# Feed-forward blocks by seven block products instead of eight, with the weight sums shared between VectorE and the DMA engines

## The chip, the cores and the metric

The kernel runs on one core of a Trainium2 chip. The metric is the device time of one execution in microseconds, the median of several. Matmuls run on TensorE (PE, with PEld for its weight loads); VectorE (DVE), ScalarE (ACT) and GpSimd (POOL) work on tiles of up to 128 partitions; SyncE (SP) issues most DMA transfers. Each engine takes its instructions in the order of the program and waits on semaphores for the others.

## The reference

One layer with 512 tokens, a width of 1024 and a feed-forward width of 2816, all in float32:

```python
def swiglu(x, w_gate, w_up, w_down):
    return (jax.nn.silu(x @ w_gate) * (x @ w_up)) @ w_down
...
    for l in range(DEPTH):
        h = rms_norm(x, norm_ffn1[l])
        x = x + 0.5 * swiglu(h, ffn1_gate[l], ffn1_up[l], ffn1_down[l])
        h = rms_norm(x, norm_mix[l])
        p = h @ w_in[l]
        ...                       # o_rwkv: a linear recurrence; o_attn: attention in a window of 128
        mixed = jnp.concatenate([o_rwkv.astype(x.dtype), o_attn.astype(x.dtype)], axis=-1)
        x = x + mixed @ w_out[l]
        h = rms_norm(x, norm_ffn2[l])
        x = x + 0.5 * swiglu(h, ffn2_gate[l], ffn2_up[l], ffn2_down[l])
    return rms_norm(x, norm_final)
```

The two feed-forward blocks, a before the mixer and b behind it, hold most of the arithmetic.

## The kernel before

A float32 product is made of three matmuls in a faster format (float32r): both factors are split into a high and a low part, and hi·hi, hi·lo and lo·hi are added up in PSUM (`mm3`, lines 455 to 457). x lies transposed, with channels on the partitions, so that eight tiles of 128x512 hold it and its split (`split_act`, 320 and 321).

A block runs over 22 columns f of 128 hidden channels. For each, gate and up take 24 matmuls apiece: the weights (128x128) are stationary and all 512 tokens move (`ffn`, 462 to 510). `gated` (516 to 520) makes silu(gate) times up, which is split again (317, 318). The down projection comes in three parts of 8, 8 and 6 hidden tiles, and adds into x from PSUM (508). The last part of block b runs in the layout of the output, with the hidden tiles stationary and the weights moving (`finish`, 548 to 550), and the last norm follows there piece by piece (553 to 569).

Weights come by SP into three raw tiles of 512 KB (`weights_load`, 402); ACT makes the high part (409) and DVE the low part (410), one or two tiles ahead of their use, driven by a list (`make_plan`, `want`, `take`). At the start, x's tiles are transposed by PE as they land (233) and products of the first column stand between the transposes (252). Statistics of the norms are matmuls of one column (341), a power by GpSimd (344) and a spread over the partitions by PE (350, 352). In the mixer, x is put away to DRAM and fetched again by GpSimd's queue (595, 601).

Of the kernel before, what the change touches and what calls it, by code (L numbers as in the profile page):

```python
# [5 lines left out]
F32 = mybir.dt.float32  # L6
# [4 lines left out]
P = 128  # L11
# [14 lines left out]
MAN = {PE, ACT, DVE}  # L26
AHEAD = 2
SPREAD = 13
MS = 8
# [7 lines left out]
MPOOL = False  # L37
MAN1 = {PE}
# [12 lines left out]
w.5.1 wd.6.1 a.4 m.7.1 zd.4 t.6 oe.3 we.5 ah.4 wd.5.1 w.7.0 u.4 ux al.4 bp.1 uv.4 te.6 g.1 wd.5.0 w.7.1 bo.1 t.5 ud.4  # L51
we.7 s.4 wd.7.0 te.5 o.4 wd.7.1 a.6 oe.4 n.4.0 ge.1 a.5 n.4.1 ah.6 q.1 t.7 al.6 ah.5 b.6 wh.0 gb.1 z.5 al.5 te.7 var.1
# [3 lines left out]
wo.5.1 wl.3 wo.4.0 xa.5 ns.3 wo.7.0 ht.3 wo.4.1 mg.3 wo.7.1 wh.4 xa.4 mh.3 wl.4 wo.6.0 ml.3 wo.6.1 xa.7 xa.6  # L56
"""
PARTS = [(0, 8), (8, 16), (16, 22)]
# [3 lines left out]
KEEP = "rg"  # L62
PACK = 1792 + 768 + 512 * sum({"r": 4, "v": 4, "g": 1, "e": 1, "O": 4, "V": 1, "w": 8}[x] for x in KEEP)
DECAY = math.exp(-0.5)

class Net:
    def __init__(self, ctx, tc, I, out):
# [10 lines left out]
        self.m2 = pool(name="m2", bufs=2)  # L78
        self.dram = pool(name="dram", bufs=1, space=bass.MemoryType.DRAM)
# [22 lines left out]

    def keep(self, x, name):
        return self.const(S) if x in KEEP else self.tile2(name)

    def consts(self):
        nc, I = self.nc, self.I
        cp = self.cp
        self.pack = cp.tile([P, PACK], F32, name="pack")
# [13 lines left out]
    def first_gain(self):  # L123
        nc = self.nc
        pt = self.psum("gain1_ps")
# [4 lines left out]
    def vectors(self):  # L130
        """The vectors over channels, one column per 128 of them."""
# [24 lines left out]
        pt = self.psum("vec_ps")  # L156
# [4 lines left out]
    def consts_mix(self):  # L161
        nc, I, cp = self.nc, self.I, self.cp
        c = self.col["mix"]
# [5 lines left out]
        # per-head one-hot columns and the block of ones per head  # L169
# [8 lines left out]
        # takes the mean of each head's channels off  # L178
        self.cent = self.const(P)
        nc.vector.scalar_tensor_tensor(self.cent, self.blk, -1.0 / 64, self.ident, ALU.mult, ALU.add)  # L180
        # [s, 0, t] = t > s; [s, 1, t] = t >= s, s = partition mod 64
# [7 lines left out]
        # 0 at the first step of each chunk  # L189
# [3 lines left out]
        # window mask  # L193
# [13 lines left out]
    def start(self, x):  # L207
        """Loads x, transposes it and makes the first operands, and the products of the first tile of the first ffn."""
        nc = self.nc
        with self.tc.manual_schedule(engines={PE, ACT, DVE, mybir.EngineType.SP}):  # L210
            self.warm()
            raws, ws = [], []
            for j in range(ND):
                if j % 2 == 0:
                    xin = self.tile4(f"xin{j}", (P, 2, 4, P))
                raws.append(xin[:, j % 2])
                nc.sync.dma_start(raws[j], x[0, :, j * P:(j + 1) * P].rearrange("(t p) c -> p t c", p=P))
                if j < 4:
                    self.first_load(ws)
# [1104 lines left out]
```

## Time and profile before

| | us |
|---|---|
| median of three runs | 1022.75 |
| lowest and highest run | 1021.14, 1022.91 |
| span of the profiled execution, first to last instruction | 1023.7 |
| PE busy in it | 1008.6 |
| DVE busy | 557.8 |
| ACT busy | 397.5 |
| POOL busy | 52.2 |

The profile is of one execution; its span is 0.95 us over the median of the runs. Shares of the page's 40 slices and its table of engines are averages over stages with different limits: block a lies from 0 to about 384 us, the mixer to about 665, block b to the end.

### The profile page before, as it was taken

The numbers are of one execution on the slowest core, as the hardware profiler recorded it, in microseconds if no ns is written. First come the engines' busy times: TensorE is split into PE (matmuls) and PEld (weight loads), VectorE is DVE, ScalarE is ACT, GpSimd is POOL, SyncE is SP. The second block draws the span as 40 slices with busy tenths as digits, with TensorE's granted clock in tenths as the row PEclk, the third lists the DMA queues.
The fourth block names the chain that finished last, engine by engine and source line by source line (L and its number), as shares of the span: only waits on it lengthen the run. The fifth ranks groups of instructions, "written<-read, shape, count | busy, mean of one in ns | idle before, by whom it ended". The sixth has DMA issues, their size and how long they took to land. (4 is left out here: it accounts for less than half of the span.)

```text
span 1023.7 us, 12876 instructions
## 1 busy us (share of the span) xinstructions
PE 1008.6 (99%) x5123; PEld 824.8 (81%) x5123; DVE 557.8 (54%) x886; ACT 397.5 (39%) x631; POOL 52.2 (5%) x84
## 2 busy tenths in 40 slices
PE   8999999999999999999999999999999999999997
PEld 6888888888888887888867788788888888888886
DVE  5644424444344568799976686644443444424445
ACT  5422212332222447864376754432222322212343
POOL 6000000000000010120010120000000000000001
PEclk8999999999999999999989899999999999999999
DMA  8333333333233352313230323223333333333322
GB/s 207 103 101 87 100 103 92 94 103 101 85 102 93 103 176 62 94 51 78 77 84 22 93 63 103 81 87 101 102 97 88 103 101 88 101 103 90 96 83 83
DMA packets 174444, 96.82 MB, mean 95 GB/s; under 512 B 12334, under 2 KB 170096, under 8 KB 174384
## 3 DMA queue, kind: packets, MB, share of 16 engines
q1 hardware_dynamic: 172032, 90.19, 30.9%
q0 software_dynamic: 2336, 5.81, 2.0%
q8 instruction: 40, 0.66, 0.3%
q14 instruction: 20, 0.16, 0.1%
q10 hardware_dynamic: 16, 0.00, 0.0%
HBM read 89.43 MB, written 4.19 MB: 91 GB/s over the span
## 5 line engine op out<-in xcount | busy, mean ns | idle before, releaser
L457 PE MATMUL bpgu<-h_o,lo_bg 128*128 128x512 f32 x176 | 69.3, 394 | 0.0
L455 PE MATMUL bpgu<-h_o,hi_bg 128*128 128x512 f32 x176 | 69.2, 393 | 0.0
L456 PE MATMUL bpgu<-h_o,hi_bg 128*128 128x512 f32 x176 | 69.0, 392 | 0.0
L455 PE MATMUL apd<-h_a,hi_ad 128*128 128x512 f32 x176 | 68.6, 390 | 0.0
L456 PE MATMUL apd<-h_a,hi_ad 128*128 128x512 f32 x176 | 68.5, 389 | 0.0
L457 PE MATMUL apd<-h_a,lo_ad 128*128 128x512 f32 x176 | 68.5, 389 | 0.0
L457 PE MATMUL bpgu<-h_o,lo_bu 128*128 128x512 f32 x176 | 68.5, 389 | 0.0
L455 PE MATMUL bpgu<-h_o,hi_bu 128*128 128x512 f32 x176 | 68.5, 389 | 0.0
L456 PE MATMUL bpgu<-h_o,hi_bu 128*128 128x512 f32 x176 | 68.5, 389 | 0.0
L457 PE MATMUL apgu<-h_x,lo_au 128*128 128x512 f32 x168 | 65.5, 390 | 0.0
L455 PE MATMUL apgu<-h_x,hi_ag 128*128 128x512 f32 x168 | 65.5, 390 | 0.0
L455 PE MATMUL apgu<-h_x,hi_au 128*128 128x512 f32 x168 | 65.4, 390 | 0.0
L456 PE MATMUL apgu<-h_x,hi_au 128*128 128x512 f32 x168 | 65.4, 389 | 0.0
L457 PE MATMUL apgu<-h_x,lo_ag 128*128 128x512 f32 x168 | 65.4, 389 | 0.0
L456 PE MATMUL apgu<-h_x,hi_ag 128*128 128x512 f32 x168 | 65.4, 389 | 0.0
L409 ACT ACTIVATE hi_bu<-raw_bu 128x1024 fp32r<-128x1024 f32 x22 | 23.4, 1061 | 87.0 <-PE bpgu L456 78.3
L409 ACT ACTIVATE hi_au<-raw_au 128x1024 fp32r<-128x1024 f32 x21 | 22.3, 1062 | 83.0 <-PE apgu L456 70.1
L516 DVE TENSOR_TENSOR sgb<-bpgu,rstd 128x512 f32<-128x512 f32 x22 | 15.2, 692 | 70.6 <-PE bpgu L457 69.4
L516 DVE TENSOR_TENSOR sga<-apgu,rstd 128x512 f32<-128x512 f32 x22 | 15.2, 691 | 69.2 <-PE apgu L457 66.4
L409 ACT ACTIVATE hi_ad<-raw_ad 128x1024 fp32r<-128x1024 f32 (+1 forms) x24 | 23.8, 991 | 74.9 <-PE apd L456 51.9
L455 PE MATMUL bpd<-h_b,hi_bd 128*128 128x512 f32 x128 | 49.8, 389 | 0.0
L456 PE MATMUL bpd<-h_b,hi_bd 128*128 128x512 f32 x128 | 49.8, 389 | 0.0
(427 smaller groups left out, 2348.3 us busy)
## 6 DMA issues: line engine op xcount, KB each, us to landing
raw_bg<-in_ffn_gate_dram SPq DMA_DIRECT2D x22, 512.0 KB, 3.8
raw_bu<-in_ffn_up_dram SPq DMA_DIRECT2D x22, 512.0 KB, 3.8
raw_ag<-in_ffn_gate_dram SPq DMA_DIRECT2D x21, 512.0 KB, 3.9
raw_au<-in_ffn_up_dram SPq DMA_DIRECT2D x21, 512.0 KB, 3.8
raw_ad<-in_ffn_down_dram SPq DMA_DIRECT2D x16, 512.0 KB, 4.0
raw_bd<-in_ffn_down_dram SPq DMA_DIRECT2D x16, 512.0 KB, 4.0
raw_o<-in_w_out_dram SPq DMA_DIRECT2D x16, 256.0 KB, 3.3
raw_ad<-in_ffn_down_dram SPq DMA_DIRECT2D x8, 384.0 KB, 3.6
```

Of the source, the lines that this page charges most:

```text
L409: nc.scalar.activation(hi[:, :n], raw[:, :n], AF.Copy)
L455: nc.tensor.matmul(ps, hi[:, k], ah, start=first, stop=False)
L456: nc.tensor.matmul(ps, hi[:, k], al, start=False, stop=False)
L457: nc.tensor.matmul(ps, lo[:, k], ah, start=False, stop=last)
L516: nc.vector.tensor_tensor(sg, pg, self.rstd, ALU.mult)
```

## The change

Both blocks are rewritten. Tokens and both other dimensions are halved, and each product of 2x2 blocks is made by seven block products (M1, M7, M2, M6, M5, M3, M4 in this order) of sums of blocks, in the form that accumulates in PSUM. Activations are stationary (128x128) and weights move, 512 columns at a time (256 in the last of six column blocks). For gate and up, the two block columns are up and gate, and the two block rows are the halves of the 1024 channels; a product has two pieces of 128x1024 weights, and each takes 12 matmuls. The hidden rows come out with tokens on the partitions; PE turns them (`hidden_turn`). The down part runs each product over six pieces.

`Stream` replaces the list of weights. `loads` issues the plain loads, by SP, and for three of four weight blocks of down by GpSimd's queue. A weight sum is made in place in a raw tile: `add` is a transfer from DRAM that accumulates, `add_here` an addition by DVE. Activation sums are additions by GpSimd. x now lies in rows (`xN`); for the mixer it is transposed by `turn_rows` in `tail_a` and `between`, at the start by `operand_turn`, and the output projection of the mixer has the activations stationary too.

```diff
+PRODUCTS = ("M1", "M7", "M2", "M6", "M5", "M3", "M4")
+LOADS, LOADS_D, HIGH, LOW, HI, LO = 9, 5, 3, 2, 5, 4
...
+    def add(self, pc, b, i, j):
+        self.nc.gpsimd.dma_start(self.raw[pc.kind, pc.c, pc.idx, b], pc.block(i, j), accum_op=ALU.add)
+
+    def add_here(self, pc, b, other):
+        a, o = (self.raw[pc.kind, pc.c, pc.idx, x] for x in (b, other))
+        self.nc.vector.tensor_tensor(a, a, o, ALU.add)
...
+            b = {"M1": "11", "M7": "12", "M2": "21", "M3": "22"}.get(pc.m)
+            if b:
+                eng = self.nc.gpsimd if pc.kind == "d" and pc.m != "M3" else by or self.nc.sync
+                eng.dma_start(self.tile(pc, b), pc.block(int(b[0]) - 1, int(b[1]) - 1))
+            if pc.m == "M7":
+                self.add(pc, "12", 1, 1)
...
+            self.nc.scalar.activation(hi, raw, AF.Copy)
...
+            self.nc.vector.tensor_tensor(lo, raw, hi.bitcast(F32), ALU.subtract)
+            self.parts[pc.q] = hi, lo
+            if pc.m == "M7":
+                self.add_here(pc, "12", "11")
+                self.add(pc, "11", 0, 1)
+            elif pc.m == "M6" and pc.kind == "gu":
+                self.add_here(pc, "12", "21")
+            elif pc.m == "M6":
+                self.add(pc, "12", 1, 0)
...
+    def mm3w(self, ps, ah, al, bh, bl, first, last):
+        mm = self.nc.tensor.matmul
+        mm(ps, ah, bh, start=first, stop=False, skip_group_check=True)
+        mm(ps, al, bh, start=False, stop=False, skip_group_check=True)
+        mm(ps, ah, bl, start=False, stop=last, skip_group_check=True)
...
+        for f in range(nf):
+            nc.tensor.transpose(pt[:, f], h[:, f * P:(f + 1) * P], self.ident)
+        nc.scalar.activation(self.hT[c][:, :, t * P:(t + 1) * P], pt, AF.Copy)
...
+        if pc.m == "M7":
+            self.ds[pc.c] = self.f.tile([P, 2, 256], F32, tag="ds", name=f"ds{pc.q}", bufs=5)[:, :pc.nk]
+            eng.tensor_tensor(self.ds[pc.c], a11, a21, ALU.subtract)
+        elif pc.m == "M6":
+            eng.tensor_tensor(a21, a22, a21, ALU.subtract)
+            eng.tensor_tensor(a11, a11, a21, ALU.add)
+        elif pc.m == "M3":
+            eng.tensor_tensor(a12, a11, a12, ALU.subtract)
...
+        for j in range(4):
+            self.turn_rows(j, gain)
+        for t in (2, 3):
+            self.row_squares(self.xN[t], t)
+        self.row_scales()
```

The start, PE, before: transposes of x (L233) and the first column's gate and up products (L252).

```order
L233 MATMUL xt_ps_131<-pack,xin_101 128x128 x4
L126 MATMUL gain_ps<-pack,gain_rows 128x8
L233 MATMUL xt_ps_144<-pack,xin_101 128x128 x4
L233 MATMUL xt_ps_152<-pack,xin_109 128x128 x4
L252 MATMUL apgu_130<-h_x_139,hi_ag_104 128x512 x2
L252 MATMUL apgu_130<-h_x_149,hi_ag_104 128x512
L233 MATMUL xt_ps_169<-pack,xin_109 128x128 x4
L252 MATMUL apgu_130<-h_x_149,hi_ag_104 128x512
L252 MATMUL apgu_130<-h_x_139,lo_ag_105 128x512
L252 MATMUL apgu_130<-h_x_149,lo_ag_105 128x512
L252 MATMUL apgu_130<-h_x_157,hi_ag_104 128x512 x2
L252 MATMUL apgu_130<-h_x_157,lo_ag_105 128x512
```

The start, PE, now: transposes (L535) and the first product (L644 to L646).

```order
L246 MATMUL gain_ps<-pack_128,gain_rows 128x8
L535 MATMUL xta_143<-pack_128,xin_106 128x128 x4
L535 MATMUL xta_153<-pack_128,xin_107 128x128 x4
L535 MATMUL xta_167<-pack_128,xin_108 128x128 x4
L535 MATMUL xta_173<-pack_128,xin_109 128x128 x4
L535 MATMUL xta_189<-pack_128,xin_106 128x128 x4
L535 MATMUL xta_195<-pack_128,xin_107 128x128 x4
L535 MATMUL xta_201<-pack_128,xin_108 128x128 x4
L535 MATMUL xta_207<-pack_128,xin_109 128x128 x4
L644 MATMUL Xa_0_236<-hia,AaM1h 128x512
L645 MATMUL Xa_0_236<-hia,AaM1l 128x512
L646 MATMUL Xa_0_236<-loa,AaM1h 128x512
```

All eight groups of transposes now stand ahead of the first product, where before five of them stood behind or between products.

The start, POOL, before: the identity for the transposes (`pack`, L112 and L113) and other constants.

```order
L1319 UNCONDITIONAL_BRANCH
L112 MEMSET pack 128x128
L118 MEMSET pack 128x32
L171 MEMSET pack 128x2
L175 MEMSET pack 128x128
L113 ISA
L113 AFFINE_SELECT pack<-pack 128x128
```

The start, POOL, now (`rawaa` are raw weight tiles, `xga` x times the norm's gain, `s3a` their difference for M7, `pack_128` at L232 to L233 the identity).

```order
L1617 UNCONDITIONAL_BRANCH
L131 DMA rawaa<-in_ffn_gate_dram 128x2x512 x2
L232 MEMSET pack_128 128x128
L233 ISA
L233 AFFINE_SELECT pack_128<-pack_128 128x128
L236 MEMSET pack_128 128x1
L238 MEMSET pack_128 128x32
L544 TENSOR_TENSOR s3a<-xga_139,xga_141 128x1024
L131 DMA rawaa<-in_ffn_gate_dram 128x2x512
```

Two accumulating transfers stand ahead of the identity, and sums of activations stand between the later ones.

Block a, POOL, before: constants, the norm's power (L344), and then nothing until x's eight transfers to DRAM behind the block (`x_spill`, the first shown).

```order
L172 MEMSET pack 64x1
L173 MEMSET pack 64x1
L201 DMA pack<-in_attn_sinks_dram 128x8
L344 TENSOR_TENSOR ms<-ms,pack 128x4
L595 DMA x_spill<-xT_167 128x512
```

The start of the down part of block a, POOL, now (L707 sums activations for M7, L144 loads a weight block, L131 accumulates into one; `r12a` is M7's sum, `r11a` the block of M1).

```order
L707 TENSOR_TENSOR ds_1873<-hTa_754 128x512
L144 DMA r12a_1890<-in_ffn_down_dram 128x2x512
L131 DMA r12a_1890<-in_ffn_down_dram 128x2x512
L614 DMA xN_227<-in_x_dram 128x1024
L614 DMA xN_228<-in_x_dram 128x1024
L614 DMA xN_229<-in_x_dram 128x1024
L614 DMA xN_230<-in_x_dram 128x1024
L707 TENSOR_TENSOR ds_1899<-hTa_1017 128x512
L144 DMA r12a_1916<-in_ffn_down_dram 128x2x512
L131 DMA r12a_1916<-in_ffn_down_dram 128x2x512
L131 DMA r11a_1672<-in_ffn_down_dram 128x2x512
```

GpSimd, which had no work here, now alternates between sums, loads and accumulating transfers; each transfer into `r12a` waits until the load ahead of it has landed, and the rows of x (`xN`) stand among them.

The passage from block a to the mixer, ACT, before: a channel tile's operand (L320) and square (L327) follow each product's weights (L409).

```order
L320 ACTIVATE h_an_2506<-xT_233,pack 128x512
L327 ACTIVATE sq_2509<-xT_233 128x512
L409 ACTIVATE hi_ad_7_2533<-raw_ad_7_2531 128x768
L320 ACTIVATE h_an_2538<-xT_249,pack 128x512
L327 ACTIVATE sq_2541<-xT_249 128x512
L409 ACTIVATE hi_in_wa<-raw_in_wa 128x1024
L320 ACTIVATE h_an_2570<-xT_257,pack 128x512
L327 ACTIVATE sq_2573<-xT_257 128x512
L409 ACTIVATE hi_in_gl<-raw_in_gl 128x1024
L320 ACTIVATE h_an_2602<-xT_259,pack 128x512
L327 ACTIVATE sq_2605<-xT_259 128x512
```

The same passage, ACT, now: the last four tiles turned by PE (`xt_m`), each with its operand (L763) and a copy (L768), and two rows' squares (L394).

```order
L763 ACTIVATE h_an_2712<-xt_m_2707,pack_128 128x512
L768 ACTIVATE xT_2715<-xt_m_2707 128x512
L763 ACTIVATE h_an_2722<-xt_m_2717,pack_128 128x512
L768 ACTIVATE xT_2715<-xt_m_2717 128x512
L763 ACTIVATE h_an_2731<-xt_m_2726,pack_128 128x512
L768 ACTIVATE xT_2734<-xt_m_2726 128x512
L763 ACTIVATE h_an_2741<-xt_m_2736,pack_128 128x512
L768 ACTIVATE xT_2734<-xt_m_2736 128x512
L394 ACTIVATE sq_2745,ss_m<-xN_229 128x1024
L394 ACTIVATE sq_2747,ss_m<-xN_230 128x1024
L475 ACTIVATE wsplit<-wraw 128x1024
L413 ACTIVATE rstd<-rstd_ps 128x512
```

Four tiles and two rows' squares now stand in one row, with no product's weights between them.

## Rows read from the trace of the kernel before

**Rows 1.** The page: busy time of each engine, share of the span, instructions.

```profile
PE 1008.6 (99%) x5123; PEld 824.8 (81%) x5123; DVE 557.8 (54%) x886; ACT 397.5 (39%) x631; POOL 52.2 (5%) x84
```

**Rows 2.** Stretches: from:to, length, busy us (x instructions) by engine, granted clock, DMA share, GB/s.

```profile
0.00:30.00 30.00, 25.36 (x107) 19.32 (x108) 19.05 (x30) 18.12 (x30) 16.22 (x46) 0.89 0.85 209
...
60.00:200.00 140.00, 140.00 (x620) 115.95 (x619) 59.80 (x70) 38.10 (x44) 0.00 (x0) 1.00 0.33 95
```

**Rows 3.** What PE waited for: us in total, times, longest.

```profile
PE xt_ps L233 <- DMA xin<-in_x_dram: 3.4, 2, 2.3
PE rstd_ps L350 <- POOL ms L344: 1.7, 1, 1.7
```

**Rows 4.** Timeline of PE in block a: start, us, engine, line; twelve starts apart.

```profile
100.19 0.39 PE L457 MATMUL apgu<-h_x,lo_au 128*128 128x512 f32 x1
...
102.91 0.39 PE L457 MATMUL apgu<-h_x,lo_au 128*128 128x512 f32 x1
```

**Rows 5.** Timeline of PE at the end of block b; thirty-five starts apart.

```profile
1012.79 0.28 PE L548 MATMUL e<-hi_be,h_b 128*128 128x256 f32 x1
...
1016.99 0.28 PE L550 MATMUL e<-hi_be,h_b 128*128 128x256 f32 x1
```

**Rows 6.** Timeline of PE, the 32 transposes of the last norm's rows.

```profile
980.51 3.65 PE L541 MATMUL xn_ps<-pack,xr 128*128 128x128 f32 x32
```

**Rows 7.** Groups by line and shape: busy us, mean ns of one, idle before.

```profile
L410 DVE TENSOR_TENSOR lo_bg<-raw_bg,hi_bg 128x1024 fp32r<-128x1024 f32 x22 | 27.0, 1225 | 41.3 <-ACT hi_bg L409 41.3
...
L409 ACT ACTIVATE hi_bu<-raw_bu 128x1024 fp32r<-128x1024 f32 x22 | 23.4, 1061 | 87.0 <-PE bpgu L456 78.3 <-PE bpd L456 8.8
...
L516 DVE TENSOR_TENSOR sgb<-bpgu,rstd 128x512 f32<-128x512 f32 x22 | 15.2, 692 | 70.6 <-PE bpgu L457 69.4 <-ACT rstd L352 1.2
...
L327 ACT ACTIVATE sq<-xT 128x512 f32<-128x512 f32 x16 | 9.2, 622 | 0.0
...
L1198 ACT ACTIVATION_READ_ACCUMULATOR scs<-scs,nm 128x1 f32 x32 | 6.1, 190 | 0.0
...
L321 DVE SCALAR_TENSOR_TENSOR h_an<-xT,pack,h_an 128x512 fp32r<-128x512 f32 x8 | 6.0, 745 | 0.0
...
L320 ACT ACTIVATE h_an<-xT,pack 128x512 fp32r<-128x512 f32 x8 | 5.8, 723 | 0.4
```

**Rows 8.** The page's DMA queues: packets, MB, share of 16 engines' span.

```profile
q1 hardware_dynamic: 172032, 90.19, 30.9%
q0 software_dynamic: 2336, 5.81, 2.0%
```

**Rows 9.** Stretches of 5 us at the start.

```profile
0.00:5.00 5.00, 3.75 (x11) 1.73 (x11) 0.57 (x2) 1.49 (x2) 4.15 (x22) 1.00 0.55 155
5.00:10.00 5.00, 1.62 (x10) 1.18 (x9) 2.33 (x4) 1.89 (x3) 4.74 (x10) 0.84 1.16 279
10.00:15.00 5.00, 5.00 (x17) 3.89 (x16) 2.71 (x5) 3.41 (x6) 3.59 (x9) 0.50 1.18 281
15.00:20.00 5.00, 5.00 (x29) 4.24 (x28) 4.30 (x8) 3.52 (x7) 3.25 (x9) 0.98 1.16 262
```

**Rows 10.** DMA issues: count, KB each, median us from issue to landing.

```profile
raw_bg<-in_ffn_gate_dram SPq DMA_DIRECT2D x22, 512.0 KB, 3.8
...
raw_be<-in_ffn_down_dram SPq DMA_DIRECT2D x6, 512.0 KB, 3.4
...
raw_au<-in_ffn_up_dram SPq DMA_DIRECT2D x2, 256.0 KB, 6.4
```

**Rows 11.** Groups of POOL by line and shape.

```profile
L344 POOL TENSOR_TENSOR ms<-ms,pack 128x4 f32<-128x4 f32 x3 | 5.8, 1928 | 60.3 <-DVE ms L343 60.3
...
L601 POOL DMA_DIRECT2D xr<-x_spill x8 | 4.4, 552 | 42.9 <-PE pv L990 41.9 <-PE in_ps_av L457 1.0
...
L191 POOL MEMSET pack<- 128x512 f32 x1 | 0.5, 533 | 0.1
```

**Rows 12.** Timeline of the last microseconds.

```profile
1017.30 0.42 DVE L553 SCALAR_TENSOR_TENSOR xn<-e,xn 128x256 f32<-128x256 f32 x1 [0.73 <-PE e L550]
...
1019.70 0.81 SPq L569 DMA_DIRECT2D out_dram<-z  x2
```

## Prediction before the run

> **What bounds the kernel now.** I read the page's busy times first. TensorE is busy 1008.6 us of 1023.7 [rows 1], so whatever shortens the time must shorten TensorE's work or the few waits around it. Then the table by stretches: in 60 to 200 us, inside the first feed-forward block, PE is busy for all 140 us, while DVE works 59.8, ACT 38.1 and the DMA engines a third of the time [rows 2]. So the two blocks are bound by matmuls alone, with more than half of every other engine free. The groups of waits show how little TensorE loses: 3.4 us for the first pieces of x, 1.7 us for the last norm's statistics [rows 3]; the rest lies before the first matmuls and after the last one. The profile's span is 1023.7 us; the runs shown have a median of 1022.75, so I make the sum against 1023.7 and take 0.95 off at the end.
>
> **What the products save.** A matmul of 512 columns takes (102.91 - 100.19) / 12 = 0.2267 us from start to start [rows 4], one of 256 columns (1016.99 - 1012.79) / 35 = 0.120 us [rows 5]. The order of the two blocks has 3150 of 512 and 36 of 256 columns before: 714.1 + 4.3 = 718.4 us. The changed one has 2604 and 336: 590.3 + 40.3 = 630.6 us. That is **-87.8 us**. The seven products need activations on both sides: hidden rows come out with tokens on the partitions and are turned back by 176 transposes, and x is turned by 64 + 32 where 64 were before, so 208 are added; 32 of them take 3.65 us [rows 6], so 208 x 0.114 = **+23.7 us**, all on TensorE. A few statistics matmuls of one column go; I count nothing for them. Pure TensorE work falls by **64.1 us**. The mixer keeps its 672 matmuls of 512 columns.
>
> **What the other engines must now do.** Per block of 512 hidden columns TensorE needs 168 x 0.2267 + 16 x 0.114 = 39.9 us. DVE has 14 weight lows and 4 block sums or operand lows of 128x1024 at 1.22 us, and about 10 operations of 128x512 at 0.69 [rows 7]: 29 us. ACT has 14 weight highs at 1.06 and some 12 shorter ones: 23 us. Both fit. Loads are 4 MB and accumulating transfers 2 MB per 39.9 us; 90.19 MB cost 30.9% of the engines' span before [rows 8], so 4 MB take about 0.34 of a block's time and 2 MB a sixth, or two sixths if a transfer that also reads its target costs twice. It fits either way. In the down part seven products take 7 x 2.72 = 19.0 us; DVE has 8 operations at 1.22 and 7 at 0.69, 14.6 us; the transfers are 2 MB and 1.5 MB. So I cost the weight sums at nothing in the middle of each part, covered by TensorE's products, and if that cover goes they cost what DVE or the DMA engines exceed.
>
> **The start: +19 us.** Before, transposes and first products stand mixed in TensorE's order. By 30 us 107 matmuls had started [rows 2]; without 7 for warming, one for the gain and 32 transposes, 67 products are 15.2 us, and the transposes 3.5, so 11.3 us of 30 were lost. Now all eight groups of transposes stand ahead of the first product, and the last needs the tenth to twelfth transfer of SP: 5 MB at about 280 GB/s [rows 9] are there at 18 us plus about 3. GpSimd builds the identity only behind two accumulating transfers, which wait until their targets have landed. VectorE, in order, does a weight sum (L135) that waits for such a transfer before it empties the later transposes. I get the first product at about 24 us. The clock then stands at its lower level, 1.2 of 2.4 GHz, for some us, as it did before in 10 to 15 us (granted 0.50) after 5 us with PE busy for 1.62 [rows 9]: at most 3.4 us lost. With stalls of about 5 us while the second and third product wait for sums on GpSimd, about 30 are lost, 19 more than before. Bounds: 8 (only x is late) to 25.
>
> **Two prices the trace does not show.** An accumulating transfer has no row. The nearest plain ones of 512 KB land in 3.4 to 3.8 us, and at the crowded start one of 256 KB took 6.4 [rows 10]. I take 4.0 since the stages in question move under half of what the DMA engines can, and keep 3.4 to 6.4. Nor has a wide two-operand operation on GpSimd: a MEMSET of 128x512, which only writes, takes 0.53, and the narrow power operation 1.93 [rows 11]. I take the middle, 1.2 us for 128x512, and about 2 for 128x1024. The trace's VectorE takes 1.23 us for 128x1024 [rows 7]; the Trainium skill (GPSIMD Engine Reference, section 3.1) gives GpSimd's tensor_tensor about twice VectorE's time, 4497 against 2293 ns for 2048 elements. By it 128x512 would be an estimated 1.1 us and 128x1024 2.2, and the sum would not move by 2 us. No run here shows it.
>
> **The down parts: +7 us each.** GpSimd, in order, does for each of the six pieces of the second product (M7): a sum of activations (1.2), the issue of a load (0.55 [rows 11]), the wait for its landing (4.0), the issue of the accumulating transfer into it (0.55), and one into the first block: some 6.3 to 6.9 us a piece. TensorE needs a piece each 2.72 us. It has M1 before it, 5.5 pieces or 15 us, so that the last M7 piece is wanted about 27 us after the up and gate part ends. GpSimd begins near that end, because its loads reuse tiles that TensorE still reads; six cycles, less what was started ahead, end at about 34.5. That leaves about 8 us; part of it hides behind the pieces already there, so I take 7, with 0 and 15 as bounds (six pieces at 8 us each would give the upper one). Queued behind GpSimd's wait are the loads of x's rows and the next sums; the waiter behind them is ACT's high part, then TensorE.
>
> **From block a to the mixer: +8 us.** Before, each channel tile's operands (ACT 0.72, DVE 0.75 [rows 7]) were made beside the next tile's products. Now four of eight tiles are turned after the last product: transposes, two ACT operations (0.72 and 0.62) and one of DVE through two PSUM buffers, about 1.9 us a tile, against 5.4 us of products that are ready; 3.4 us stay. Then the last two rows' squares on ACT (2 x 1.25, a 128x1024 at 1.06 and 0.19 for the accumulator [rows 7]), GpSimd's power (1.93 [rows 11]) and the spread, against 2.7 us of products: 4.8 us. Bounds 3 to 12. **From the mixer to block b: +5 us** by the same kind of chain (turn, first split, norm), three stalls of 1 to 5 us less the 1.7 us of before [rows 3]; bounds 2 to 10. **The end: +2 us**: the last product closes two rows of 1024 instead of a half row, so squares, power, scaling and two transfers come behind; before it was 1017.3 to 1023.7 [rows 5, 12].
>
> **Sum.** -64.1 + 19 + 14 + 8 + 5 + 2 = -16.1; 1023.7 - 16.1 - 0.95 = **1007 us**. Own range 990 to 1020.
>
> **Rivals.** *The waits hide.* If the start loses only what x's arrival costs (+8), M7's pieces come in time, and the two passages cost 3 and 2, the end 2: 15 us instead of 48, 974 us (963 to 988). For it: DVE, ACT and DMA are idle over half the time [rows 2]. Against it: the order is fixed per engine, and GpSimd's waits stand in front of others' inputs.
>
> *The accumulating transfer lands late, and the result is slower.* The place is GpSimd's cycle in M7 of both down parts: every us of landing over 4.0 adds one to each of six pieces in two blocks, and about two at the start: 14 us per us. The gain of 16 is gone at 4.0 + 1.15 = 5.2 us. At 6.4, the highest row, it is +34: 1041 (1025 to 1060). For it: a transfer that must also read its target; against it: 3.4 to 3.8 in calm stretches [rows 10].
>
> *VectorE and GpSimd exclude each other.* In a down part, DVE's 14.6 us of 19.0 and GpSimd's four sums of 1.2 then make 19.4, more than TensorE's time. The price lies between 0 and all 24 sums, 29 us a block; a third, 9 each, gives 1025 (1012 to 1040). In before GpSimd has no wide operation, so no row speaks for or against it. The Trainium skill (SBUF — State Buffer, section SBUF: two separate sides) says that a GpSimd operation that reads SBUF and a VectorE operation with two SBUF inputs lock each other out for a whole instruction; it is this rival, and no run here shows it. That the change leaves the eighth product in is excluded by the counts of its order.
>
> **How the numbers follow.** Forecast 0.48, hidden waits 0.22, late landing 0.20, exclusion 0.08, and 0.02 for a loss of another kind. A measurement here can tell 0.2%, 2 us. Faster by more: 0.46 of the forecast's, 0.22, 0.02 of the late landing and 0.02 of the exclusion: 0.72. Within 0.2%: 0.02 + 0.01 + 0.02 = 0.05. Slower: 0.17 + 0.04 + 0.02 = 0.23. For 8 in 10 the range goes from the middle of the hidden case, 968, to that of the late landing, 1045.
>
> **What would show it.** In the changed profile: products of 512 columns still 0.227 us apart; first product at about 24 us; in each down part some 7 us of PE idle with ACT's high of a M7 piece, or GpSimd's transfer, as releaser; 8 us before the mixer's first tiles are done; accumulating transfers that land in about 4 us. The prediction is wrong if PE shows no idle time in the down parts (then 974), if those transfers take over 5.2 us, if DVE's or GpSimd's operations there are stretched when they overlap, or if PE waits in the middle of up and gate, which I cost at nothing.

## The result and the profile after

The changed kernel takes **1112.03 us** (median of 4 runs, 1108.99 to 1115.37), the kernel before 1022.39 beside it: the ratio is 1.0891, with a 95% interval of 1.086 to 1.0922. The forecast was 1007, with a range up to 1045. The profiled execution has a span of 1113.7 us and a mean granted clock of 0.934, where before had 1023.7 and 0.988.

The page of the changed kernel, engines and DMA queues (answers to [rows 1] and [rows 8]):

```profile
PE 993.2 (89%) x5053; PEld 800.4 (72%) x5053; DVE 779.1 (70%) x1046; ACT 570.3 (51%) x891; POOL 255.6 (23%) x258
...
q0 software_dynamic: 30608, 69.25, 28.8%
q1 hardware_dynamic: 58224, 70.26, 19.8%
```

PE is busy 993.2 us, 15 less than before, but its work was worked out at 944.5 (1008.6 less 64.1). The 49 us between go with stretches at a lower granted clock: the two down parts alone, at 0.86, are 39 us over their work. Another 120 us of the span are idle. GpSimd's queue (q0) now moves as much as the hardware queue (q1), and takes half as much time again for it.

The stages of the changed kernel, from the first starts of their products (up and gate of a with its start, down of a, the mixer with its passages, up and gate of b, down of b). Columns as in [rows 2]:

```profile
0.00:261.00 261.00, 236.82 (x1130) 195.86 (x1130) 172.32 (x178) 139.34 (x183) 54.90 (x60) 0.97 0.59 155
261.00:420.00 159.00, 126.80 (x487) 99.16 (x486) 111.49 (x116) 64.66 (x95) 64.90 (x70) 0.86 0.56 135
420.00:718.00 298.00, 283.70 (x1884) 222.04 (x1883) 223.61 (x465) 172.50 (x344) 32.24 (x35) 0.95 0.32 92
718.00:950.00 232.00, 223.35 (x1089) 187.21 (x1087) 162.43 (x164) 128.34 (x168) 42.55 (x36) 0.99 0.56 141
950.00:1105.00 155.00, 122.54 (x470) 96.13 (x469) 105.97 (x119) 63.42 (x100) 59.94 (x55) 0.86 0.54 130
```

The two down parts, 261 to 420 and 950 to 1105, have PE busy for 127 and 123 us at a granted clock of 0.86, where the products need 104.7 (462 matmuls of 0.2267 us). There lies most of the loss. The steady middle of up and gate came out as forecast. Three stretches of 10 us of the changed kernel show it beside the second product (M7) and the fourth (M6) of the down part (x in brackets is instructions):

```profile
190.00:200.00 10.00, 10.00 (x50) 8.30 (x49) 7.64 (x9) 6.14 (x9) 0.00 (x0) 1.00 0.91 243
...
290.00:300.00 10.00, 4.63 (x11) 3.06 (x10) 3.05 (x3) 1.57 (x2) 4.07 (x5) 0.67 0.77 159
...
350.00:360.00 10.00, 5.45 (x24) 4.15 (x23) 10.00 (x6) 4.63 (x6) 9.00 (x9) 0.93 0.81 155
```

In 190 to 200 PE is full, and DVE and ACT have room, as the forecast had it. In 290 to 300 nothing is full: every engine waits for another. In 350 to 360 DVE is busy for all 10 us with six instructions, one of which takes 7.68 us (shown below).

What PE waited for in the changed kernel (us, times, longest; [rows 3] was 3.4 and 1.7 us in all):

```profile
PE Qbd L644 <- ACT dd L570: 23.6, 4, 6.8
PE Qad L644 <- ACT dd L570: 18.2, 5, 5.4
PE gain_ps L246 <- POOL pack L233: 10.7, 1, 10.7
PE Xad L644 <- DVE xN L752: 7.5, 1, 7.5
PE Xbd L644 <- DVE xN L752: 6.6, 1, 6.6
PE Yb L646 <- DVE lob L164: 6.6, 1, 6.6
```

`Q..d` is the PSUM of M7 and M4 in the down part, `X..d` that of M1, M6, M5 and M3. So of some 32 us that PE is idle in each down part, 18 and 24 fall on M7 (PE's waits from 280 to 324 and from 968 to 1020 us) and 7 lie between M6 and M5, behind VectorE. The named releaser of the first two rows is ACT's high of a sum of activations (`dd`). That is one step short of the cause, since ACT itself waited. The chain of one piece of M7, from GpSimd to ACT to PE, in three timelines of the changed kernel (start, us, engine, line, idle before and its releaser):

```profile
277.75 1.23 POOL L131 DMA_DIRECT2D r12a<-in_ffn_down_dram  x1 [7.33 <-DMA r12a<-in_ffn_down_dram]
278.51 1.73 POOL L131 DMA_DIRECT2D r11a<-in_ffn_down_dram  x1
279.28 2.27 POOL L707 TENSOR_TENSOR ds<-hTa 128x512 f32<-128x512 f32 x1
280.82 1.42 POOL L144 DMA_DIRECT2D r12a<-in_ffn_down_dram  x1
288.28 1.19 POOL L131 DMA_DIRECT2D r12a<-in_ffn_down_dram  x1 [6.04 <-DMA r12a<-in_ffn_down_dram]
```

```profile
283.74 1.06 ACT L155 ACTIVATE hia<-r12a 128x1024 fp32r<-128x1024 f32 x1 [8.40 <-DMA r12a<-in_ffn_down_dram]
284.70 0.61 ACT L570 ACTIVATE dd<-ds 128x512 fp32r<-128x512 f32 x1
294.20 1.06 ACT L155 ACTIVATE hia<-r12a 128x1024 fp32r<-128x1024 f32 x1 [8.88 <-DMA r12a<-in_ffn_down_dram]
```

```profile
285.37 0.50 PE L644 MATMUL Qad<-hia,dd 128*128 128x512 f32 x1 [1.98 <-ACT dd L570]
...
295.83 0.80 PE L644 MATMUL Qad<-hia,dd 128*128 128x512 f32 x1 [5.37 <-ACT dd L570]
```

GpSimd waits 7.33 and 6.04 us for the plain load of `r12a`, issues the accumulating transfer into it at 277.75 and 288.28, one into `r11a`, makes a sum, and issues the next load, which stands in its queue behind both accumulating ones. ACT's high of `r12a` waits 8.4 and 8.9 us until the accumulating transfer has landed, and ACT's next instruction, the high of the activations, stands behind it. PE gets these pieces 10.5 us apart, where it needs one each 2.72.

The waits of 7 us for VectorE (`Xad`, `Xbd`) are of another kind. VectorE, GpSimd and PE of the changed kernel around 352 us, in this order:

```profile
328.54 0.68 DVE L571 TENSOR_TENSOR dd<-hTa,dd 128x512 fp32r<-128x512 f32 x1
...
352.23 7.68 DVE L571 TENSOR_TENSOR dd<-hTa,dd 128x512 fp32r<-128x512 f32 x1
...
362.09 1.27 DVE L752 SCALAR_TENSOR_TENSOR xN<-Xad,xN 128x512 f32<-128x512 f32 x2
```

```profile
352.34 8.13 POOL L712 TENSOR_TENSOR hTa<-hTa 128x512 f32<-128x512 f32 x6
```

```profile
362.91 0.76 PE L644 MATMUL Xad<-hia,dd 128*128 128x512 f32 x1 [7.46 <-DVE xN L752]
```

An operation of VectorE that takes 0.68 us at 328.54 took 7.68 us at 352.23, about as long as six sums of GpSimd in a row. Behind it on VectorE stood a weight low, one more operand low and the emptying of PSUM (L752), and PE waited 7.46 us for that.

### The profile page after: what moved, and what is told of

Same layout as the page of the kernel before. It is cut to its first block, busy times and chain, and to the rows that moved or that the text cites. A ratio compares the mean times of both kernels' runs of the same rounds, so it can differ in the third digit from the quotient of the medians.

```text
span 1113.7 us, 13481 instructions
## 1 busy us (share of the span) xinstructions
PE 993.2 (89%) x5053; PEld 800.4 (72%) x5053; DVE 779.1 (70%) x1046; ACT 570.3 (51%) x891; POOL 255.6 (23%) x258
## 3 DMA queue, kind: packets, MB, share of 16 engines
q0 software_dynamic: 30608, 69.25, 28.8%
## 4 chain that ended last, share of the span: by engine, by line
PE 62%; issue 11%; DVE 9%; DMA 7%; POOL 6%; ACT 3%; POOLq 0%; DVEq 0%; ACTq 0%
PE Xb L646 3%; PE Xb L644 3%; PE Xb L645 3%; PE Xa L644 2%; PE Xa L646 2%; PE Xa L645 2%; DMA r12b<-in_ffn_down_dram 2%; DMA r12a<-in_ffn_down_dram 2%; PE Qb L646 2%; PE Qb L644 2%; PE Qb L645 2%; DVE dd L571 1%; PE wo L644 1%; PE wo L646 1%; PE gram L1009 1%
## 5 line engine op out<-in xcount | busy, mean ns | idle before, releaser
L131 POOL DMA_DIRECT2D rawab<-in_ffn_gate_dram x22 | 26.9, 1253 | 202.8 <-ACT hTb L693 98.6
L164 DVE TENSOR_TENSOR loa<-rawaa,hia 128x1024 fp32r<-128x1024 f32 x55 | 67.4, 1231 | 8.6 <-PE Qa L646 5.4
L164 DVE TENSOR_TENSOR lob<-rawab,hib 128x1024 fp32r<-128x1024 f32 x55 | 66.9, 1222 | 8.1 <-PE Qb L646 5.3
L155 ACT ACTIVATE hia<-rawaa 128x1024 fp32r<-128x1024 f32 x55 | 57.7, 1053 | 25.9 <-PE Ya L645 15.9
L155 ACT ACTIVATE hib<-rawab 128x1024 fp32r<-128x1024 f32 x55 | 57.8, 1053 | 25.6 <-PE Yb L645 15.9
L131 POOL DMA_DIRECT2D rawaa<-in_ffn_gate_dram x22 | 27.0, 1251 | 184.2 <-ACT hTa L693 100.1
L571 DVE TENSOR_TENSOR dd<-ds,dd 128x512 fp32r<-128x512 f32 (+1 forms) x12 | 10.5, 873 | 55.5 <-ACT dd L570 55.5
L644 PE MATMUL Xad<-hia,dd 128*128 128x512 f32 x88 | 36.3, 412 | 7.5 <-DVE xN L752 7.5
L644 PE MATMUL Qbd<-hib,dd 128*128 128x512 f32 x44 | 21.7, 494 | 23.6 <-ACT dd L570 23.6
L644 PE MATMUL Xbd<-hib,dd 128*128 128x512 f32 x88 | 36.1, 411 | 7.2 <-DVE xN L752 6.6
L645 PE MATMUL Xad<-hia,dd 128*128 128x512 f32 x88 | 36.5, 415 | 2.9 <-DVE dd L571 2.1
L644 PE MATMUL Qad<-hia,dd 128*128 128x512 f32 x44 | 21.7, 492 | 18.2 <-ACT dd L570 18.2
L645 PE MATMUL Xbd<-hib,dd 128*128 128x512 f32 x88 | 35.8, 406 | 1.4 <-DVE dd L571 1.4
L646 PE MATMUL Xad<-loa,dd 128*128 128x512 f32 x88 | 35.8, 407 | 0.0
L646 PE MATMUL Xbd<-lob,dd 128*128 128x512 f32 x88 | 35.7, 406 | 0.0
L571 DVE TENSOR_TENSOR dd<-hTb,dd 128x512 fp32r<-128x512 f32 (+1 forms) x31 | 30.8, 997 | 5.8 <-ACT dd L570 5.8
L571 DVE TENSOR_TENSOR dd<-hTa,dd 128x512 fp32r<-128x512 f32 (+1 forms) x31 | 31.1, 1005 | 5.5 <-ACT dd L570 5.5
```

The source lines that it names most:

```text
L131: self.nc.gpsimd.dma_start(self.raw[pc.kind, pc.c, pc.idx, b], pc.block(i, j), accum_op=ALU.add)
L155: self.nc.scalar.activation(hi, raw, AF.Copy)
L164: self.nc.vector.tensor_tensor(lo, raw, hi.bitcast(F32), ALU.subtract)
L571: nc.vector.tensor_tensor(lo, src, hi.bitcast(F32), ALU.subtract)
L644: mm(ps, ah, bh, start=first, stop=False, skip_group_check=True)
L645: mm(ps, al, bh, start=False, stop=False, skip_group_check=True)
```

## The experiments

Each kernel is the changed one with the edits shown; ratios are to the kernel before, with 95% intervals, where several rounds were run. Durations of a stage are worked out from the first starts of its products in the view by tile.

### Who paces the second product: GpSimd's row, or the accumulating transfer

```diff
-                eng = self.nc.gpsimd if pc.kind == "d" and pc.m != "M3" else by or self.nc.sync
+                eng = self.nc.gpsimd if pc.kind == "d" and pc.m not in ("M3", "M7") else by or self.nc.sync
```

> The changed kernel with one edit: in the down parts the plain loads of the second product's weight block (M7, r12) are issued by SP instead of GpSimd's queue. Theory A, the M7 pieces are paced by GpSimd's own row (sum, load, wait for the landing, accumulating transfer), 10.4 us a piece (277.75, 288.28, 298.60 us in the changed profile): the loads land ahead, a piece costs GpSimd about 3.5 us, M7 shrinks from 43 to about 20 us in each block, and the time falls from 1112 to about 1065. Theory B, the accumulating transfer's own landing (6 us and more) paces them: the pieces stay at 6.5 us or more, and the time stays above 1090.

Measured: 1072.08 us, ratio 1.0484 (1.0446 to 1.0522), 40 less than the change. The matmuls of M7 and then of M2 (`Qad`, `Yad`), first of the changed kernel and then of this one; the numbers behind the colon are duration, and first and last start:

```profile
L644 PE MATMUL Qad<-hia,dd x44: 389/397/795, 280.5 to 418.0; 128*128 128x512 f32 x44
```

```profile
L644 PE MATMUL Yad<-hia,dd x22: 389/389/628, 323.4 to 338.2; 128*128 128x512 f32 x22
```

```profile
L644 PE MATMUL Qad<-hia,dd x44: 388/390/796, 283.4 to 402.3; 128*128 128x512 f32 x44
```

```profile
L644 PE MATMUL Yad<-hia,dd x22: 387/390/629, 305.0 to 325.0; 128*128 128x512 f32 x22
```

From the first product of M7 to the first of M2 it is 323.4 - 280.5 = 42.9 us before the edit and 305.0 - 283.4 = 21.6 with it; in block b it is 50.9 and 22.3. A piece every 3.9 us is less than one landing of an accumulating transfer, so B falls: those transfers overlap. All six loads of M7 in block a, which GpSimd had issued one by one from 249.51 to 299.35 us, now go out together on SP:

```profile
249.32 4.75 SPq L144 DMA_DIRECT2D r12a<-in_ffn_down_dram  x6
```

They take no less time to land: the median of SP's full loads into `r12a` is 8.8 us, where GpSimd's transfers into it, loads and accumulating ones together, took 4.1 to 8.0 before the edit. So what paced M7 was not the landing as such, but GpSimd waiting for each landing before it went on to the next piece.

### Do VectorE and GpSimd lock each other out

```diff
     def down_sums(self, pc):
-        eng = self.nc.gpsimd
+        eng = self.nc.vector
```

> The changed kernel with one edit: the sums of hidden activations in the down parts (L707 to L712) are made by VectorE instead of GpSimd. Theory C, VectorE and GpSimd lock each other out: VectorE's 128x512 operand lows (mean 1118 ns) return to about 690, the one that took 7.68 us beside six sums of GpSimd goes with PE's wait of 7.5 us in each block, and GpSimd's M7 pieces lose 1.3 to 2.2 us each: about 1070. Rival, no lock, the stretched records are an artefact: VectorE has 16 us a block more to do, nothing comes back, 1105 to 1125.

Measured: 1090.61 us, ratio 1.0674 (1.064 to 1.0708), 21 less than the change. Groups of VectorE (line, shape, count, busy us, mean ns), of the changed kernel and of this one:

```profile
L571 DVE TENSOR_TENSOR dd<-hTa,dd 128x512 fp32r<-128x512 f32 x26 | 29.0, 1118 | 4.1 <-ACT dd L570 4.1
...
L164 DVE TENSOR_TENSOR loa<-r12a,hia 128x1024 fp32r<-128x1024 f32 x15 | 22.8, 1523 | 1.6 <-PE Xad L646 1.6
```

```profile
L164 DVE TENSOR_TENSOR loa<-r12a,hia 128x1024 fp32r<-128x1024 f32 x15 | 18.3, 1220 | 1.5 <-PE Xad L646 1.5
...
L571 DVE TENSOR_TENSOR dd<-hTa,dd 128x512 fp32r<-128x512 f32 x26 | 17.8, 686 | 5.3 <-ACT dd L570 5.3
```

Without sums on GpSimd the means are 686 and 1220 ns, close to the kernel before's for such shapes [rows 7], and PE's waits of 7.5 and 6.6 us behind L752 are in neither block's list. That GpSimd's sums hold VectorE up is shown. One part of the expectation missed: M7 was to become shorter by GpSimd's sums and did not (43.8 us). GpSimd's accumulating transfers into `r12a` in this kernel:

```profile
279.03 1.23 POOL L131 DMA_DIRECT2D r12a<-in_ffn_down_dram  x1 [9.00 <-DMA r12a<-in_ffn_down_dram]
...
289.29 1.19 POOL L131 DMA_DIRECT2D r12a<-in_ffn_down_dram  x1 [7.01 <-DMA r12a<-in_ffn_down_dram]
```

They stand 10.3 us apart, as before (10.5); the wait for the load grew by 1.7 and 1.0 us, about what the sum no longer took (1.5 from start to start). So the sum did not set M7's pace. The load, issued earlier, landed hardly earlier, which fits a load held up by the two accumulating transfers issued ahead of it; whether by their place in GpSimd's queue or by the DMA engines that all queues share, no run separates.

Both edits together:

> Both edits, M7's loads by SP and the sums of hidden activations by VectorE. If A and C are separate causes, their gains add up apart from the part of the M7 piece that both shorten: about 1035 us. If one hides the other, it is no faster than the better of the two.

Measured: 1045.09 us, ratio 1.0245 (1.02 to 1.029). That is 67 less than the change, where the single gains add up to 61: two separate causes, neither of which hides the other.

### What accumulating costs the DMA engines

```diff
-        self.nc.gpsimd.dma_start(self.raw[pc.kind, pc.c, pc.idx, b], pc.block(i, j), accum_op=ALU.add)
+        self.nc.gpsimd.dma_start(self.raw[pc.kind, pc.c, pc.idx, b], pc.block(i, j))
```

> The changed kernel with every accumulating transfer replaced by a plain one of the same bytes on the same queue (the weight sums made by DMA are left out, and the block is overwritten instead). Theory D, adding to the target makes the transfer slow: landings of the transfers into rawaa and r12a fall from 7.4 and 6.0 us to about 4, and the time falls by 20 us or more. Rival, the landing is long because they queue behind other transfers of GpSimd's queue: landings stay within 1 us and the time within 10 us of 1112.

The kernel leaves out the weight sums that the DMA engines make; only its time counts. Measured: 1070.21 us (one run), 42 less; M7 took 33.0 us in block a, with GpSimd's row as it was. DMA issues (count, KB, us to landing) of the changed kernel, and queue and issues of this one:

```profile
rawaa<-in_ffn_gate_dram POOLq DMA_DIRECT2D x22, 512.0 KB, 7.4
...
r12a<-in_ffn_down_dram POOLq DMA_DIRECT2D x15, 512.0 KB, 6.0
```

```profile
q0 software_dynamic: 19728, 69.25, 18.9%
...
rawaa<-in_ffn_gate_dram POOLq DMA_DIRECT2D x22, 512.0 KB, 4.8
...
r12a<-in_ffn_down_dram POOLq DMA_DIRECT2D x15, 512.0 KB, 4.0
```

Theory D stands: 7.4 and 6.0 us become 4.8 and 4.0 (the group of `r12a` mixes loads and accumulating transfers, that of `rawaa` has accumulating ones alone). GpSimd's queue takes 18.9% of 1068.5 us for the same 69.25 MB, 201.9 us, where accumulating took 28.8% of 1113.7, 320.7 us. By the order 40.4 of the 69.25 MB accumulate. At 201.9 / 69.25 = 2.92 us per MB for the plain rest, the accumulating ones took (320.7 - 28.9 x 2.92) / 40.4 = 5.85 us per MB: twice a plain transfer. These 42 us and the 40 of the moved loads overlap, since both shorten M7; on top of the other edits, accumulating is worth 17.5 us (the last run below).

### The starts of the blocks

Three runs: the constants ahead of the first transfers (`ident_first`), the operands' sums of up and gate by VectorE (`opsums_dve`), and both on top of the two edits above (`start_too`).

```diff
         self.warm()
+        self.consts()
...
         load(3, 1)
-        self.consts()
```
```diff
     def operand_sum(self, m, eng=None):
-        eng = eng or self.nc.gpsimd
+        eng = eng or self.nc.vector
```

> The changed kernel with one edit: GpSimd builds the identity ahead of its first accumulating transfers instead of behind them. If the start is set by the identity, the first product moves from 21.4 to about 15 us (the first pieces of x and weights land at 5 to 12 us) and the time falls by 4 to 7: about 1106. If x's last pieces set it, the first product stays above 19 us and the time within 3 of 1112.

Measured: 1102.18 us, ratio 1.0773 (1.0746 to 1.08), 10 less, though the first product did not move. PE at the start, of the changed kernel and of this one:

```profile
15.29 6.33 PE L535 MATMUL xta<-pack,xin 128*128 128x128 f32 x32
21.38 0.48 PE L644 MATMUL Xa<-hia,AaM1h 128*128 128x512 f32 x1
```

```profile
9.98 1.97 PE L535 MATMUL xta<-pack,xin 128*128 128x128 f32 x8 [3.51 <-DMA xin<-in_x_dram]
```

The transposes start at 9.98 us instead of 15.29, but the last ones still wait for x, and the first product comes at 21.9. The gain came later: in ACT's row M7's operand high stands ahead of a weight high of M7. It began at 17.32 us instead of 26.84, and PE's waits of 4.1 and 2.8 us for M7's weights are gone. By the fourth product (M6) 7 of the 10 us are there: it starts at 49.1 us instead of 56.1. So x's last pieces set the first product, and yet the time moved by more than that branch of the expectation allowed, for another reason.

> The changed kernel with one edit: the sums of the up and gate operands (L544 to L549) by VectorE instead of GpSimd. If the third product's waits (Ya 5.0, Yb 6.6 us) come from VectorE waiting for ACT's operand high that waits for three sums of 2.4 us on GpSimd, they vanish: 1112 less 12 of waiting and some 8 of low clock, about 1092. If VectorE has no room, 1105 or more.

Measured: 1096.98 us, ratio 1.0727 (1.0698 to 1.0755), 15 less; the third product's waits of 5.0 and 6.6 us (`Ya` in block a, `Yb` in block b) are gone, and M6 begins 8.2 us (a) and 7.6 us (b) sooner after the first product. In the changed kernel GpSimd made these sums in 2.4 us each, one in 2.9 (its timeline), and VectorE's operation beside the last one took 2.40 instead of 1.22:

```profile
24.41 2.40 POOL L544 TENSOR_TENSOR s3a<-xga,xga 128x1024 f32<-128x1024 f32 x1 [9.27 <-DVE xga L537]
...
45.49 2.36 POOL L549 TENSOR_TENSOR xga<-xga,xga 128x1024 f32<-128x1024 f32 x1
```

```profile
46.53 2.40 DVE L568 SCALAR_TENSOR_TENSOR AaM6l<-xga,AaM6h 128x1024 fp32r<-128x1024 f32 x1 [6.43 <-ACT AaM6h L567]
```

> The changed kernel with four edits: M7's loads by SP, sums of hidden activations by VectorE, GpSimd's constants (the identity) built ahead of the first transfers, and the sums of the up and gate operands (L544 to L549) by VectorE. The first two alone gave 1045. If the waits at the start of each block are GpSimd's row (identity 10.7 us, third product 5.0 and 6.6 us, second product 4.0 and 3.2 us, each followed by some us of TensorE at 1.2 GHz), this gives 1012 to 1022, a little faster than the kernel before. If the weight transfers pace those starts, the waits change their names and the time stays at 1035 or more.

Measured: 1024.54 us, ratio 1.002 (1.0004 to 1.0036), a little over the expected 1022. The four single gains are 40.0 + 21.4 + 9.9 + 15.1 = 86.4 us, and together they are 87.5: the gains add up.

### A version that beats both

Three more edits were tried on these four. The first (`start_late`) moves the transposes of x's second half of channels behind the first piece of M1, where `second_half` is called.

```diff
-        for h in range(2):
-            for t in range(4):
-                self.operand_turn(xin[t], t, h, gain)
...
+        for t in range(4):
+            self.operand_turn(xin[t], t, 0, gain)
...
+    def second_half(self):
+        for t in range(4):
+            self.operand_turn(self.xin[t], t, 1, self.gain1)
```

The other two belong to the passage from block a to the mixer (`best` and later): the last two rows' squares stand ahead of the last four turned tiles, and the mixer's first low-rank product comes one step later.

```diff
+        for t in (2, 3):
+            self.row_squares(self.xN[t], t)
+        self.row_scales()
         for j in range(4):
             self.turn_rows(j, gain)
-        for t in (2, 3):
-            self.row_squares(self.xN[t], t)
-        self.row_scales()
...
-         (("side", 2), "lora", 0), (("side", 3), "lora", 1),
+         (("side", 3), "lora", 0), (("side", 3), "lora", 1),
```

> The four edits of the run before (1024.5 us), and one more: the transposes of x's second half of channels stand behind the first piece of the first product, as the kernel before mixed them, instead of ahead of it. In the run before PE waited 9.2 us in four places for x's pieces and began its first product at 21.7 us. If the order on PE is what is left of the start, the first product begins at 14 to 16 us and the time is 1017 to 1020. If the weights or the operand splits set it, the waits move to the second product and the time stays at 1022 to 1026.

Measured: 1028.36 us, ratio 1.0076 (1.0055 to 1.0098): slower than without it. The first product began at 11.7 us, ten earlier, but PE then waited in the second product:

```profile
35.35 0.80 PE L652 MATMUL Qa<-loa,AaM7h 128*128 128x512 f32 x1 [6.39 <-DVE loa L164]
```

> As the run above, and two edits at the passage from block a to the mixer: the squares of the last two rows stand ahead of the last four turned tiles, and the first low-rank product of the mixer one step later. PE waited 2.8 us for the power and 4.7 us for the low-rank operand there, both with the clock at its lower level behind it. If those waits are the order's, the time falls by 6 to 10 more, to 1008 to 1013, faster than the kernel before; if the chain of turned tiles sets the passage, by 3 or less.

Measured: 1015.85 us, ratio 0.9949 (0.9931 to 0.9967). The passage's edits brought 12.5 us, more than expected; PE's waits of 2.8 us for the norm's power and 4.7 us for the low-rank operand, which the kernel at 1024.5 us had, are gone. The wait of the start is VectorE's row in this kernel: the scale of the norm (L405) waits for ACT's squares, and the weight low that PE needs (L164) stands behind it.

```profile
30.59 0.17 DVE L405 TENSOR_SCALAR ss_a<-ss_a 128x4 f32<-128x4 f32 x1 [3.80 <-ACT sq L398]
...
33.22 1.22 DVE L164 TENSOR_TENSOR loa<-rawaa,hia 128x1024 fp32r<-128x1024 f32 x1
```

> The four edits that gave 1024.5 us, and the two edits of the passage (squares first, low-rank product a step later), without the later transposes of x that came out slower (1028.4). If the passage's edits are worth the 12.5 us that they brought on top of the later transposes, this gives 1010 to 1014. If part of the 12.5 was an interplay with the start, 1016 or more.

Measured: **1011.11 us**, ratio 0.9892 (0.9875 to 0.9909): faster than the kernel before by 1.1%, without the later transposes. The passage's edits bring 13.4 us here, so they do not depend on the start.

The next kernel is the one at 1015.9 us with the statistics of x's rows moved behind the first piece of M2:

```diff
             self.operand_turn(self.xin[t], t, 1, self.gain1)
-        for t in range(4):
-            self.row_squares(self.xin[t], t)
-        self.row_scales()
         self.operand_split("M2")
+    def statistics(self):
+        for t in range(4):
+            self.row_squares(self.xin[t], t)
+        self.row_scales()
```

> The edits of the run at 1015.9 us, and the squares and scales of x's rows moved behind the first piece of the third product. With the later transposes the first product began at 10.9 us instead of 21.7, but VectorE's scale waited for four squares on ACT (until 30.6 us) ahead of the second product's weight low, and PE waited 7.1 us for it at the lower clock. If the statistics in VectorE's row are what ate the earlier start, PE's 7.1 us wait goes and the time falls by 8 to 14, to 1002 to 1008. If the accumulating transfer into the second product's block (landed at about 21 to 25 us) sets it, by 4 or less.

Measured: 1013.64 us, ratio 0.9912 (0.9895 to 0.9928). PE's 7.1 us wait fell to 1.6, but the time by only 2.2: the expectation of 8 to 14 missed. With the first product at 11.5 us (this kernel) or at 21.3 (`best_two`), PE's wait for M7's second weight low ends at the same moment, 30.4 and 30.8 us. Two things are left ahead of that low. ACT's highs of M7's blocks still wait 5.3 and 3.0 us for the accumulating transfers, and the second is done at 26.5 us; the low follows only at 29.1, since the emptying of x's later transposes and M2's operand low stand ahead of it in VectorE's row. Which of the two paces the start is open: no run separates them.

> As the run above with every accumulating transfer replaced by a plain one of the same bytes (the weight sums made by DMA are left out). The DMA engines' share is about 1.0 for 60 us around the second product of each down part. If what is left there (M7 at 21.6 us instead of 15) is the DMA engines' time for accumulating, M7 shrinks to 15 to 17 us in block a and the time falls by 12 to 20. If it is the order on GpSimd, ACT or DVE, M7 stays above 20 us and the time within 6.

This kernel, too, leaves out the sums made by the DMA engines. Measured: 998.36 us (one run), 17.5 less than the run at 1015.9, and M7 in block a takes 17.1 us instead of 23.1. M7's products need 15, so 6 of the 8 us that M7 still loses there go with accumulating. Three stages of the fastest kernel (`best_two`): down of a, the mixer, down of b:

```profile
247.00:376.00 129.00, 117.07 (x489) 91.20 (x488) 102.01 (x139) 64.98 (x96) 30.06 (x44) 0.96 0.63 152
376.00:658.00 282.00, 275.28 (x1884) 217.47 (x1882) 222.60 (x464) 171.75 (x344) 32.34 (x35) 0.99 0.33 98
...
882.00:1000.00 118.00, 111.07 (x471) 86.13 (x469) 101.49 (x141) 62.72 (x99) 25.68 (x28) 1.00 0.63 159
```

Its granted clock is 0.96 and 1.00 in the down parts, and PE's busy time 958.5 us in all. The first product still waits for x (9.9 us in four places); the down part of a takes 129 us instead of 159, that of b 118 instead of 155.

## Why the prediction was wrong

Each stage's measured time (the stretches above, with exact bounds 260.7, 420.0, 717.6, 949.7 and 1104.8 us) stands beside PE's work in it, worked out with [rows 4 to 6]:

| stage | work | measured | loss | forecast loss |
|---|---|---|---|---|
| start, up and gate of a | 224.3 | 260.7 | 36 | 30 |
| down of a | 106.5 | 159.3 | 53 | 7 |
| mixer and both passages | 278.6 | 297.6 | 19 | 13 |
| up and gate of b | 220.6 | 232.1 | 12 | 0 |
| down of b | 104.7 | 155.1 | 50 | 7 |

(The mixer's work is the 273.1 us that it took before from the first product of its first tile, at 376.1 us, to the first of block b, at 649.2, and 48 more transposes; the bounds of about 384 and 665 given with the profile before are late.) The end took 8.9 us, with 8.4 forecast. Work, forecast losses and end add up to 1000 and not 1007.6: the other 7.5 us are losses of the kernel before, which the forecast kept.

**Right:** the products' cost, the steady part of up and gate (PE full from 160 to 200 us, DVE 28.1 and ACT 22.0 of the 40), the start in its size (lost 36 for 30), the two passages' kind of wait, and the end. In the start two errors cancel in part: the first product came at 21.4 us for 24 (behind the identity, and without that wait x holds it to 21.9), and the stalls of the second and third product behind it were 12 us for 5. In the passage's sum four tiles at 1.9 us less 5.4 us of products are 2.2 us and not 3.4.

**Wrong, and most of the 106 us between 1007.6 and 1113.7:** the step "The down parts: +7 us each". They lost 53 and 50 us. The mechanism, GpSimd's row pacing M7, was right. The term that failed first is "the wait for its landing (4.0)", with 6.4 as its highest row: GpSimd waited 5.9 to 7.3 us for the load in the middle of M7 of block a and up to 9.7 in block b, with accumulating transfers under way ahead of it that each cost the DMA engines twice a plain one. The prediction priced the load as if alone. So GpSimd's cycle was 10.3 to 10.5 us a piece in the middle of block a's M7, not 6.3 to 6.9, and M7 took 43 us in block a and 51 in b. Moving the loads, and with them the waiting, gave 40 us back.

Two terms of the down parts stood at nothing in the sum. One is the clock: PE at intervals is at its lower level, 1.2 of 2.4 GHz (granted 0.67 as a mean over 290 to 300), and PE's busy time in the two down parts was 21 and 18 us over the work; in the fastest kernel, where M7 takes 23 and 21 us, the granted clock there is 0.96 and 1.00. The other is VectorE held up by GpSimd's sums: PE's 7.5 and 6.6 us between M6 and M5. ACT's high of the activations, which the step names as the waiter, costs little by itself: it ends 0.5 us behind the weight high that the same product needs.

A third term at nothing lay outside: up and gate of b lost 12 us, since its third product waits for GpSimd's operand sums (6.6 us) as that of block a does. The prediction priced such stalls in block a's start alone; making those sums on VectorE gave 15 us, half of it in each block.

**Rivals that were both true.** The late landing had 0.20 and the price 14 us for each us over 4.0; at 6.0 that gives 28 us, 1035, a quarter of what came. It put the price on the wrong transfer: in GpSimd's row stands the wait for the plain load, and the accumulating transfers, which landed in some 6 us, overlap when nothing waits between them. The exclusion of VectorE and GpSimd had 0.08. It was priced by a share of the sums' time; what it cost is 21 us by the run without those sums, near the 18 of the prediction. That nearness is luck in part, since a third of the sums' time was a guess and the run also gives VectorE more to do. The error was to treat it as an alternative: it adds to the others. The Trainium skill (SBUF — State Buffer, section SBUF: two separate sides) says that the loser of the shared port pair waits for the whole instruction of the other; the trace agrees, and shows more: VectorE's 0.68 us operation waited through six instructions in a row, 7.68 us.

**The middle at nothing.** The weight sums in the middle of up and gate cost nothing, as said. The narrower claim that the transfers fit "either way" held in the mean (a DMA share of 0.63 over 160 to 200 us) but not around M7: in the kernel with both edits of the down parts (1045 us) the share was 0.95 and 1.08 in the two halves of 265 to 305 us. That the DMA engines themselves bound M7 there is borne out by the last run, in which plain transfers took M7 from 23.1 to 17.1 us.

**Left open:** whether the accumulating transfers' double time comes from reading their target or from how they are split into packets (30608 packets of GpSimd's queue against 19728 for the same bytes); no run tells these apart. Open as well is whether M7's plain load was late by its place in GpSimd's queue or by the shared DMA engines.

## What to carry to other kernels

When a change adds a new kind of transfer, price not one transfer but the cycle of the engine that issues it: what it waits for in its own row, and which transfers are under way ahead of the load that it waits for. A wait and the issue of the next load belong on different engines; moving the loads alone was worth 40 us here. Fewer products on the bound engine do not pay while some piece of each product passes through a row of waits: the same 64 us of saved TensorE work gave 9% more time, and after six edits of placement 1.1% less.

## What the runs showed of the hardware

- An accumulating transfer from DRAM took the DMA engines about twice the time of a plain one for the same bytes (5.85 against 2.92 us per MB, as a mean over the 16 engines), and landed 1.8 to 2.6 us later (medians of 512 KB into `rawaa` and `rawab`: 7.4 and 6.6 us, plain 4.8).
- A sum of two 128x512 tiles on GpSimd took 1.31 us at its shortest and 1.5 to 2.1 in the means of its groups beside VectorE; of 128x1024 it took 2.4. The forecast had taken 1.2 and 2. The Trainium skill (GPSIMD Engine Reference, section 3.1) has 4497 ns for 2048 elements, by which 128x1024 would be an estimated 2.2 us; the trace is near it.
- One operation of VectorE with both inputs in SBUF can wait through a series of GpSimd operations: 7.68 us for 0.68.
- Idle gaps of 4 to 7 us in a product with PE busy for 4.6 of 10 us went with a granted clock of 0.67, and in each down part PE's busy time was some 18 to 21 us longer than its work, on top of 32 us of idle time.
